# One step of a hybrid recurrence/attention block: where the chunk sums of the modulation, the second set of keys and the weight parts stand in the order of work

## Chip, cores and metric

The kernel runs on one core of one Trainium2 chip, as one launch. The metric is the device time of that launch in microseconds (us). Three runs of the kernel before gave 2032.13, 2034.22 and 2036.62 us; the median, 2034.22 us, is the time to compare with.

The core's engines work side by side, each through its own queue in order: TensorE (PE in the profile, with its weight loads as PEld), VectorE (DVE), ScalarE (ACT), GpSimd (POOL), and SyncE (SP), whose queue issues most of the DMAs. Matrix products go to PSUM, of which this kernel has eight banks in use under three tags: three "g", three "s" and two "t".

## What is computed

One trunk layer for 256 context tokens and 1024 latent tokens, width 1024, all in float32. Cut to what matters here:

```python
m = silu(cond) @ w_ada + b_ada            # 6 x 1024 modulation values, for two conditions
h = rms_norm(x) * (1 + sc1) + sh1
z = h @ w_in                              # 1024 x 5376: recurrence, attention, gates
q, k = rms_norm per head (+ rotary)
o_a = softmax(q k^T / 8) v                # 8 heads, 2 key heads, latents see 512 cached keys too
s   = dec * s + k_end^T v                 # gated recurrence, 4 heads, two directions, by chunks
o_h = intra + inter, rms_norm, silu gate
x   = x + g1 * ((gate0 * o_h @ w_ho + gate1 * o_a @ w_ao) @ w_out)
x   = x + g2 * (relu(norm2(x) @ w_ff1) ** 2 @ w_ff2)
```

The vector `m` has 48 columns of 128 values for each condition. Sixteen of them (`sh1`, `sc1`) are needed at the start; the other thirty-two are made beside the attention and the recurrence.

## The kernel before

Each float32 product is made of three passes in a rounded format (high by high, high by low, low by high), so every operand is first split into a high and a low part: one ACT copy and one DVE subtraction (`split`, L318 and L319). In the part of the kernel that the change touches, PE is given its order by hand: what the program issues first, PE does first. DVE, ACT, POOL and SP are ordered by a planner that follows the program's order, raised or lowered by `tc.high_priority(offset=...)` and held back by `tc.issue_after(x)`, which keeps an instruction's place behind x.

**Filler.** The projection `z = h @ w_in` for eighteen column groups of 256 is a generator, `with_ada`, that issues three matmuls (a "triple", L351 to L353 or L368 to L370) at each step. `attention` and `hgrn` draw on it between their own steps, by shares of the total and not by time. Groups 3, 4, 8 and 9 have 80 triples each (token-major), the others two halves of 24.

**Attention.** Thirty-two latent units of six steps, then eight context units of one step, 200 steps in all. `events` gives each action of a unit a place on one axis: scores (L856), exponentials (L868), at each step `trans` (four transposes L888 of the probabilities into a bank "t", split by ACT and DVE at L891), and later `value` (L902, L903). All events are sorted by place and carried out with filler between them. The keys of the second group of heads are loaded (`load_k`) 8.95, 8.85 and 7.9 steps ahead of step 96.

**Chunk sums.** Twelve chunks of two columns of `m` are made beside the filler's groups 1 to 9. `begin` loads a chunk of `w_ada` (a tile of ring "wraw", two places, shared with the groups' weights) and lets POOL multiply and add it up into `ACC`, one pair of buffers for all chunks (`ada_sum`, L197 to L204). `end` puts eight small matmuls with ones (L209) on PE, into a bank "t", and an ACT copy (L211); a third action puts one transpose (L215) into another bank "t" and a DVE addition (L217). All three stand at shares of a group: in a token-major group `begin` at 0.02, `end` at 0.45 and the last at 0.49, then again 0.5, 0.93 and 0.97; in the others 0.25, 0.93 and 0.97. The group after the current one is loaded at 0.05 of a token-major group.

**Recurrence.** Twenty-four units (4 heads, two directions, three token tiles). Each has a long preparation on DVE, POOL and ACT, scores (L1133), `states_` with the products L1145 into a bank "s" and a chain of two or four updates on DVE (L1154), `out`, `keys_t` and, for every second direction, `gate`. Filler runs between them.

**Weight parts.** `Group.part` splits a half of a group's weights with its place held behind `behind`, a pair that `trans` sets to the last ACT and DVE splits of the probabilities. Nothing sets `behind` in the recurrence. The split weights lie in ring "wsp" with six places, three halves.

## Time and profile before

| | |
|---|---|
| median of three runs | 2034.22 us |
| the profiled execution's own time | 2033.12 us |
| its span in the profile | 2031.1 us |
| PE busy | 1999.8 us, 98% of the span |
| DVE busy | 1346.1 us, 66% |
| ACT busy | 941.9 us, 46% |
| POOL busy | 584.7 us, 29% |
| granted TensorE clock, mean | 0.998 |

The span is counted from the first to the last instruction of the program; 2.0 us of the execution lie around it. Attention runs from about 160 to 700 us, the recurrence from about 700 to 980 us. A busy share is counted from starts and modelled ends of matmuls, which overlap by up to 0.2 us, so a pause of PE shorter than that doesn't show as idle.

### The profile page before, as it was taken

The page shows a single profiled execution, that of the slowest core. Times are in us where ns is not written, and L with a number is a line of the kernel's source. Part 1 is how long each engine was busy: PE and PEld are TensorE (multiplying, and loading weights), DVE is VectorE, ACT ScalarE, POOL GpSimd, SP SyncE. Part 2 cuts the span into 40 slices and gives each one's busy share as a digit, 9 for nine tenths or more (in the row PEclk, how much of TensorE's full clock was granted, in tenths as well). Part 3 has the DMA queues.
Part 4 walks back from the last instruction along what each step waited for, and adds up shares of the span by engine and source line. Part 5 has one row for each costly group of instructions (what it writes and reads, how often), then busy time and mean ns, then how long its engine had stood idle before and what let it go on. Part 6 is the DMA issues. An engine that isn't in the chain of part 4 may idle for free.

```text
span 2031.1 us, 32983 instructions
## 1 busy us (share of the span) xinstructions
PE 1999.8 (98%) x12183; PEld 1729.0 (85%) x12183; DVE 1346.1 (66%) x2469; ACT 941.9 (46%) x1974; POOL 584.7 (29%) x651
## 2 busy tenths in 40 slices
PE   7999999999999999999999999999999999999998
PEld 5898899988889988888888889988888888888886
DVE  5955656555665789887445535876666666577786
ACT  4735565555565423333412236754554544333443
POOL 1571337523325555554022101222212200000120
PEclk9999999999999999999999999999999999999999
DMA  9472221322122355553844435854444489455764
GB/s 319 136 226 76 79 81 63 110 91 77 55 73 92 123 180 157 187 160 125 261 135 148 148 110 160 258 173 147 157 153 148 154 313 351 126 173 174 233 237 134
DMA packets 222562, 320.00 MB, mean 158 GB/s; under 512 B 19097, under 2 KB 140737, under 8 KB 222401
## 3 DMA queue, kind: packets, MB, share of 16 engines
q1 hardware_dynamic: 209920, 277.99, 42.9%
q0 software_dynamic: 12480, 39.91, 5.3%
q8 instruction: 96, 1.57, 0.3%
q14 instruction: 66, 0.53, 0.1%
HBM read 232.05 MB, written 85.78 MB: 156 GB/s over the span
## 4 chain that ended last, share of the span: by engine, by line
PE 92%; DVE 3%; DMA 2%; ACT 1%; issue 1%; SPq 0%; POOL 0%; POOLq 0%; DVEq 0%; ACTq 0%
PE ps_g L351 8%; PE ps_g L353 8%; PE ps_g L352 8%; PE ps_s L856 4%; PE ps_t L888 4%; PE ps_g L903 2%; PE ps_g L368 2%; PE ps_g L902 2%; PE ps_g L369 2%; PE ps_g L370 2%; PE ps_g L1844 2%; PE ps_g L1845 2%; PE ps_g L1843 2%; PE ps_s L1683 2%; PE ps_s L1684 2%; PE ps_s L1682 2%
## 5 line engine op out<-in xcount | busy, mean ns | idle before, releaser
L351 PE MATMUL ps_g<-hs,wsp 128*128 128x512 f32 (+1 forms) x896 | 322.2, 360 | 0.0
L353 PE MATMUL ps_g<-hs,wsp 128*128 128x512 f32 (+1 forms) x896 | 309.2, 345 | 0.0
L352 PE MATMUL ps_g<-hs,wsp 128*128 128x512 f32 (+1 forms) x896 | 309.0, 345 | 0.0
L318 ACT ACTIVATE wsp<-wraw 128x512 fp32r<-128x512 f32 (+1 forms) x186 | 116.7, 667 | 227.3 <-PE ps_g L352 95.9
L319 DVE TENSOR_TENSOR wsp<-wraw,wsp 128x512 fp32r<-128x512 f32 (+1 forms) x186 | 149.0, 822 | 89.6 <-ACT wsp L318 89.3
L857 DVE TENSOR_REDUCE mx<-ps_s 128x1 f32<-128x512 f32 (+1 forms) x208 | 137.6, 667 | 105.1 <-PE ps_s L856 103.6
L891 DVE TENSOR_TENSOR pTl<-ps_t,pTh 128x512 fp32r<-128x512 f32 x200 | 136.4, 684 | 88.8 <-ACT pTh L891 88.5
L353 PEld LDWEIGHTS ps_g<-hs,wsp 128*128 128x128 f32 x896 | 169.3, 189 | 21.6
L351 PEld LDWEIGHTS ps_g<-hs,wsp 128*128 128x128 f32 x896 | 169.6, 189 | 19.7 <-issue 4.8
L352 PEld LDWEIGHTS ps_g<-hs,wsp 128*128 128x128 f32 x896 | 169.9, 190 | 14.4
L891 ACT ACTIVATE pTh<-ps_t 128x512 fp32r<-128x512 f32 x200 | 118.8, 603 | 125.1 <-PE ps_t L888 124.7
L318 ACT ACTIVATE ah<-ar 128x640 fp32r<-128x640 f32 (+1 forms) x112 | 80.9, 723 | 187.5 <-PE ps_g L1844 102.3
L868 ACT ACTIVATE pexp<-ps_s,ngm 128x512 f32<-128x512 f32 (+1 forms) x208 | 137.6, 671 | 46.3 <-DVE ngm L861 46.0
L319 DVE TENSOR_TENSOR ah<-ar,ah 128x640 fp32r<-128x640 f32 (+1 forms) x112 | 92.0, 822 | 76.6 <-ACT ah L318 76.3
L856 PE MATMUL ps_s<-Kl,Ql 128*128 128x512 f32 (+1 forms) x416 | 130.2, 411 | 1.1 <-DMA Kl<-KS 1.0
L888 PE MATMUL ps_t<-ident,pexp 128*128 128x128 f32 x800 | 120.3, 273 | 1.9 <-ACT ev L211 1.3
L368 PE MATMUL ps_g<-wsp,hs 128*128 128x256 f32 x400 | 116.3, 291 | 0.0
L370 PE MATMUL ps_g<-wsp,hs 128*128 128x256 f32 x400 | 112.8, 282 | 0.0
L369 PE MATMUL ps_g<-wsp,hs 128*128 128x256 f32 x400 | 112.7, 282 | 0.0
L888 PEld LDWEIGHTS ps_t<-ident,pexp 128*128 128x128 f32 x800 | 94.1, 140 | 12.5 <-ACT ev L211 2.1
L903 PE MATMUL ps_g<-pTl,Vl 128*128 128x256 f32 x400 | 104.0, 282 | 0.2
L902 PE MATMUL ps_g<-pTh,Vl 128*128 128x256 f32 x400 | 104.1, 282 | 0.0
(448 smaller groups left out, 5411.9 us busy)
## 6 DMA issues: line engine op xcount, KB each, us to landing
ar<-AF SPq DMA_DIRECT2D x112, 320.0 KB, 3.4
wraw<-in_w_ff SPq DMA_DIRECT2D x32, 1024.0 KB, 6.4
wr<-in_w_ff SPq DMA_DIRECT2D x128, 256.0 KB, 4.6
wraw<-in_w_in SPq DMA_DIRECT2D x18, 1024.0 KB, 5.6
wraw<-in_w_ada SPq DMA_DIRECT2D x16, 1024.0 KB, 5.3
AF<-a POOLq DMA_DIRECT2D x48, 256.0 KB, 2.7
AF<-t POOLq DMA_DIRECT2D x48, 256.0 KB, 2.4
wa<-in_w_ada SPq DMA_DIRECT2D x32, 256.0 KB, 5.9
```

What stands on the lines that cost most here:

```text
L318: s_.activation(hi, raw, AF.Copy)
L319: return v.tensor_tensor(lo, raw, f32(hi), op=ALU.subtract)
L351: pe.matmul(out, hi[:, k, :], mh, start=(first and k == 0), stop=False)
L352: pe.matmul(out, hi[:, k, :], ml, start=False, stop=False)
L353: pe.matmul(out, lo[:, k, :], mh, start=False, stop=(last and k == kcs - 1))
L368: pe.matmul(po[:, bb, :], mh[:, off:off + P], wh[:, k % 4, :], start=(k == 0), stop=False)
L369: pe.matmul(po[:, bb, :], mh[:, off:off + P], wl[:, k % 4, :], start=False, stop=False)
L370: pe.matmul(po[:, bb, :], ml[:, off:off + P], wh[:, k % 4, :], start=False, stop=(k == KC - 1))
L856: pe.matmul(pq[:, 0:n], self.qh[:, q0:q0 + P], K[self.g][var][self.kts[i]], start=(var == 0), stop=(var == 1))
L888: pe.transpose(pt[:, a, j * P:(j + 1) * P], self.Ps[j][i][:, b * P:(b + 1) * P], ident)
L891: behind[:] = s_.activation(hi, pt, AF.Copy), v.tensor_tensor(lo, pt, f32(hi), op=ALU.subtract)
L902: pe.matmul(pv[:, 0:256], V[self.g][kg][:, b, :], hi[:, a, :], start=(k == 0), stop=False)
```

## The change

Three edits.

1. `end` no longer puts its matmuls on PE: it leaves them in `waiting`. A new event, `beat`, stands 0.01 ahead of `trans` at steps 0 and 3 of each latent unit and at the step of each context unit. A beat carries out one thing: the transpose that is left from the beat before, or else the eight matmuls of the oldest chunk waiting. If a `begin` came while a chunk was waiting, it is put off (`starts`) and carried out in the same beat, behind the matmuls. After the attention all that is left is carried out.
2. The second set of keys is loaded 9.95, 9.85 and 8.95 steps ahead of step 96; the first set as before.
3. `behind` is also set by each update of a state (L1154) and by the addition that ends `out` in the second direction (L1177), together with `copied[0]`, the last copy of transposed keys on ACT. So in the recurrence the splits of weights stand behind these.

```diff
@@ Unit.events
             for p2 in range(self.nstep):
+                if p2 % 3 == 0:
+                    out.append((p2 - 0.01, beat, ()))
                 out.append((p2, self.trans, (p2,)))
@@ attention
-                    events += [(s0 - a, load_k, (u.g, kg)) for kg, a in enumerate((8.95, 8.85, 7.9))]
+                    events += [(s0 - a, load_k, (u.g, kg)) for kg, a in enumerate((9.95, 9.85, 8.95) if s0 else (8.95, 8.85, 7.9))]
@@ HUnit.states_
-                    v.scalar_tensor_tensor(dst, st, self.dec[:, b:b + 1], kv[:, b, :], op0=ALU.mult, op1=ALU.add)
+                    behind[:] = copied[0], v.scalar_tensor_tensor(dst, st, self.dec[:, b:b + 1], kv[:, b, :], op0=ALU.mult, op1=ALU.add)
@@ HUnit.out
-                v.tensor_tensor(o[:, 0:nb], po[:, 0:nb], fwd.o[:, 0:nb], op=ALU.add)
+                behind[:] = copied[0], v.tensor_tensor(o[:, 0:nb], po[:, 0:nb], fwd.o[:, 0:nb], op=ALU.add)
@@ build
+    waiting, starts, lasts = [], [], []
+
+    def beat():
+
+        if lasts:
+            lasts.pop()()
+        elif waiting:
+            lasts.append(waiting.pop()())
+            if starts:
+                starts.pop()()
+
@@ with_ada
                 def begin():
-                    late.append(ada_sum(ahead.pop(0), ACC))
+                    if waiting:
+                        starts.append(begin)
+                    else:
+                        late.append(ada_sum(ahead.pop(0), ACC))
 
                 def end():
-                    late.append(late.pop()())
-                acts = [(0.02, begin), (0.45, end), (0.49, lambda: late.pop()())] if grp.tok else []
+                    waiting.append(late.pop())
+                acts = [(0.02, begin), (0.45, end)] if grp.tok else []
                 if nxt and nxt in groups[:10]:
-                    acts += [(0.5 if grp.tok else 0.25, begin), (0.93, end), (0.97, lambda: late.pop()())]
+                    acts += [(0.5 if grp.tok else 0.25, begin), (0.93, end)]
@@ build
     attention(fz)
+    while waiting or lasts:
+        beat()
```

## The prediction, made before the changed kernel was run

> **What bounds the kernel now.** I read the page's busy shares first, then the chain that ended last, then the stretches of attention and recurrence, then what PE waited for.

> ```profile
> PE 1999.8 (98%) x12183; PEld 1729.0 (85%) x12183; DVE 1346.1 (66%) x2469; ACT 941.9 (46%) x1974; POOL 584.7 (29%) x651
> ...
> PE 92%; DVE 3%; DMA 2%; ACT 1%; issue 1%; SPq 0%; POOL 0%; POOLq 0%; DVEq 0%; ACTq 0%
> ```
> ```profile
> 160.00:700.00 540.00, 535.19 (x3779) 487.27 (x3778) 325.50 (x622) 313.86 (x753) 216.08 (x221) 1.00 0.26 83
> 700.00:980.00 280.00, 278.03 (x2264) 236.68 (x2263) 228.89 (x535) 88.03 (x226) 144.00 (x155) 1.00 0.51 162
> ```
> ```profile
> PE ps_s L1145 <- issue: 2.0, 2, 1.2
> ...
> PE ps_t L209 <- DVE pTl L891: 1.3, 1, 1.3
> ...
> PE ps_t L888 <- ACT ev L211: 1.3, 3, 0.4
> PE ps_s L856 <- DMA Kl<-KS: 1.0, 2, 0.9
> ...
> PE ps_t L888 <- DVE modc L217: 0.5, 2, 0.3
> ...
> PE ps_t L215 <- ACT ev L211: 0.2, 1, 0.2
> ```

> PE is the bound. In the stretch of attention (160 to 700 us) it idles 4.8 us, in the recurrence 2.0 us; the change takes no work off PE, so what it can win lies in these two stretches. The waits name nearly all of it: 3.3 us at seven places around the chunk sums (1.3 + 1.3 + 0.5 + 0.2), 1.0 us for keys, 2.0 us ahead of L1145. The true loss is a little more, because the modelled end of a matmul overlaps the next one:

> ```profile
> 528.79 0.27 PE L352 MATMUL ps_g<-hs,wsp 128*128 128x256 f32 x1
> 528.91 0.28 PE L353 MATMUL ps_g<-hs,wsp 128*128 128x256 f32 x1
> 530.52 0.30 PE L209 MATMUL ps_t<-sums,ones 128*32 128x128 f32 x2 [1.33 <-DVE pTl L891]
> ```

> From start to start this is 1.61 us where the neighbour of that shape started 0.12 before, so 1.49 is lost and 1.33 shown: 0.16 more at each place. That makes about 4.4 us for the sums (3.3 + 7 x 0.16), 1.3 for the keys, 2.3 before L1145. **8.0 us, 0.4%, is the most that can be won.**

> **Part 1a, the sums' old waits: 4.4 us go, about 2.4 come back.** A beat puts the sum's bank "t" between two `trans`, and there are two such banks. Whether `trans` then waits depends on how long before it the previous `trans` was split off. One unit's step 3 and the next unit's step 0, with the DVE split of the step before each:

> ```profile
> 282.84 0.60 PE L888 MATMUL ps_t<-ident,pexp 128*128 128x128 f32 x4
> 282.96 0.68 DVE L891 TENSOR_TENSOR pTl<-ps_t,pTh 128x512 fp32r<-128x512 f32 x1
> ...
> 289.45 0.68 DVE L891 TENSOR_TENSOR pTl<-ps_t,pTh 128x512 fp32r<-128x512 f32 x1
> 290.98 0.60 PE L888 MATMUL ps_t<-ident,pexp 128*128 128x128 f32 x4
> ```

> At step 0 the previous split ended at 290.13, 0.85 us before: both banks are free and a beat costs nothing. At step 3 it ends at 283.64, 0.8 us after `trans` began; with a beat ahead, `trans` waits for that or for the beat's own bank, whichever is first. What the latter costs, the trace shows:

> ```profile
> 272.67 0.66 PE L888 MATMUL ps_t<-ident,pexp 128*128 128x128 f32 x4 [0.26 <-DVE modc L217]
> ```

> 0.26 and the hidden 0.16 are 0.4 us lost; behind the ACT copy (1.3 us at three places) it is 0.6. I take 0.5. Setting the old places of the twelve sums against the beats, I find about ten of the 24 beats at a step 3. Half of these waiting 0.5 gives 2.4 us; the ends are 0 and 5. Net gain 2.0.

> **Part 1b, the last sum: a new wait of about 7.6 us.** The beat makes a sum late, and a sum that is late holds up the next chunk on POOL, since `ACC` is one buffer.

> ```profile
> 657.51 0.62 POOL L197 TENSOR_TENSOR sums<-wraw,ada_l 128x256 f32<-128x256 f32 x1 [9.18 <-PE ps_t L209]
> ...
> 677.88 0.74 POOL L204 TENSOR_TENSOR pvt<-wraw 128x256 f32<-128x256 f32 x1
> ```

> A chunk takes POOL 21.1 us (657.51 to 678.62), and starts 0.5 us after the sum before it. For the others, whose places lie farther apart, there is room. For the last there isn't:

> ```profile
> 652.94 0.60 PE L888 MATMUL ps_t<-ident,pexp 128*128 128x128 f32 x4
> ...
> 657.01 0.30 PE L209 MATMUL ps_t<-sums,ones 128*32 128x128 f32 x2
> ...
> 664.51 0.60 PE L888 MATMUL ps_t<-ident,pexp 128*128 128x128 f32 x4
> ...
> 681.78 0.30 PE L209 MATMUL ps_t<-sums,ones 128*32 128x128 f32 x2
> ...
> 682.95 0.60 PE L888 MATMUL ps_t<-ident,pexp 128*128 128x128 f32 x4
> ```

> The eleventh sum's `end` is at 657.01, behind the beat at the step 3 of 652.94. The next beat is that of the first context unit, at 664.51, 7.5 us later. The last sum's `end` is at 681.78; its beat follows at 682.95. So POOL would have 683.0 - 665.0 = 18.0 us for 21.1 us of work: at least 3.1 us late.

> The ring of raw weights makes it worse. In that stretch the filler does so many triples:

> ```profile
> 657.20:661.20 4.00, 1.89 (x7) 1.32 (x7) 1.00 0.33 93
> 661.20:663.00 1.80, 0.86 (x4) 0.57 (x3) 1.00 0.43 155
> ```

> The `end` at 0.93 of group 8 stands at triple 75 of 80, so the last `begin` (0.02 of group 9) comes at the 7th triple behind it, before 661.2, and group 10's load (0.05) at the 10th, before 663.0 (one of the four is counted twice). The sum before still waits, so this `begin` is put off to 664.51, past the load. The two now take their ring places in the other order. Which places these are:

> ```profile
> 648.36 0.39 SPq L101 DMA_DIRECT2D wraw<-in_w_ada  x1
> ...
> 664.14 0.49 SPq L101 DMA_DIRECT2D wraw<-in_w_in  x1
> ```
> ```profile
> 662.06 2.05 DVE L319 TENSOR_TENSOR wsp<-wraw,wsp 128x512 fp32r<-128x512 f32 x2
> ```
> ```profile
> wraw<-in_w_ada SPq DMA_DIRECT2D x16, 1024.0 KB, 5.3
> ```

> Today the chunk is loaded at 648.36 and group 10's weights at 664.14, as soon as DVE has split group 9's last weights (662.06 + 2.05). Swapped, the chunk's load goes at 664.14, lands 5.3 later at 669.4, and POOL ends at 690.5. PE stands at L209 from 683.0 to 690.6: 7.6 us (3.1 if the places don't swap). Behind it in PE's queue stand the next transposes, the last values and all filler; ACT and DVE wait for those. SP's queue only exchanges two loads.

> **The clock.** A pause of that length costs more than itself:

> ```profile
> 16.60:20.00 3.40, 1.70 (x23) 1.08 (x22) 0.94 (x3) 1.89 (x4) 0.00 (x0) 1.00 1.09 349
> 20.00:23.40 3.40, 3.40 (x9) 2.64 (x9) 2.68 (x4) 1.54 (x3) 0.00 (x0) 0.50 1.09 360
> ...
> 2027.00:2031.00 4.00, 0.00 (x0) 0.00 (x0) 0.00 (x0) 0.00 (x0) 0.00 (x0) 0.51 0.36 133
> ```

> After 3.4 us in which PE was half idle the granted clock was 0.50 for the next 3.4 us, with PE fully busy; and at the end of the kernel it is 0.51 from 2027 on. 3.4 us at half speed lose 1.7 us. I add 1.7; the ends are 0 and 3.4. [...]

> **Part 2, the keys: 1.3 us go.**

> ```profile
> 395.38 2.49 SPq L101 DMA_DIRECT2D Kl<-KS  x4
> ```
> ```profile
> 401.83 0.47 PE L856 MATMUL ps_s<-Kl,Ql 128*128 128x512 f32 x1 [0.86 <-DMA Kl<-KS]
> ```

> The last four loads are issued from 395.38 to 397.87 and PE waits for them at 401.83. One step is about 2.7 us (540 us, 200 steps), more than the 1.3 lost. The cover is a free place in ring "X", where two exponentials now come behind the keys; if SP finds none earlier, nothing is won. Bounds 0 and 1.3; I take 1.3.

> **Part 3, weight parts behind updates: 2.3 us go, about 1.5 come.**

> ```profile
> 788.76 2.12 DVE L319 TENSOR_TENSOR wsp<-wraw,wsp 128x512 fp32r<-128x512 f32 x2
> 790.80 0.34 DVE L1154 SCALAR_TENSOR_TENSOR ust<-ust,udec,ps_s 128x128 f32<-128x128 f32 x1
> ```
> ```profile
> 777.64 1.06 PE L1145 MATMUL ps_s<-uv,ukt 128*128 128x128 f32 x8
> ```
> ```profile
> L319 DVE TENSOR_TENSOR wsp<-wraw,wsp x30: 626/681/1541, 704.0 to 969.9; 128x512 fp32r<-128x512 f32 x30
> ```

> Two splits of a later half's weights stand ahead of the last update of a chain, and PE's next L1145 waits for the bank. Held back, they leave the chain. But then a half's splits come only when the filler asks for them, half a half ahead of use, behind the updates of that moment. Thirty splits, two to a half, are 15 halves in 280 us, so that lead is some 9 us. And DVE runs late: this chain's products were done by 778.7 and its last update at 791.1. DVE is busy 228.89 of 280 us here. A few waits of PE for weights, 0.5 us each, are likely: 1.5 in all; ends 0 and 7. Net gain 0.8.

> **Sum.** Against the profiled execution's 2033.12 us (span 2031.1 and 2.0 around it): -2.0 - 1.3 - 0.8 + 7.6 + 1.7 = +5.2, so 2038.3. The median of the runs, 2034.22, is 1.1 above that execution: **2039.4 us**. A measurement of this kernel can tell 0.2% (4.1 us) from no change, so this is just beyond it.

> **Rivals.**
> *The ring doesn't swap.* [...] For it: the swap hangs on the 1.5 us between 663.0 and the beat. Chance 0.13.
> *No new wait, faster.* If PE takes the eleventh sum before about 661.5 and its load is not put off, POOL is done by 683 and only the gains stay: 2034.2 - 4.1 = 2030.1, a little less where step 3 costs less. It decides at the beat of 664.51: 3 us earlier and nothing waits. Against it: places are shares of the filler, and don't drift. Chance 0.20.
> *The weights become the wait.* Three or four halves of the recurrence each 2 us late: 5.5 more, 2045. For it: DVE's lag of 12 us against a lead of 9. Chance 0.12.
> *The clock stays whole*: 2037.7. Chance 0.09.
> *The forecast*: 0.46, from 2036 to 2043.

> **Chances.** Slower by over 0.2% (above 2038.3): three quarters of the forecast and the weights, 0.46. Within: the rest of the forecast 0.12, no swap 0.13, whole clock 0.09, the dearer end of no wait 0.03, 0.37. Faster: 0.17. The range takes in the end of no wait and most of the late weights: 2029 to 2044.

> **What would show it.** One L209 near 683 with a wait for POOL of 7 to 8 us, the last load of a chunk behind a load of group 10, and a stretch of granted clock below 1 behind it; L888 waits gone at step 0 and some 0.4 at step 3; no wait at L856 near 400; no split between updates of one chain, and perhaps L351 waiting for DVE. If L209 waits nowhere, the count of triples or of POOL's time is wrong.

## The result, and the profile after

The changed kernel takes 2049.67 us (median of six runs, 2046.01 to 2051.3) against 2033.49 us of the kernel before, measured beside it (six runs, 2032.13 to 2036.62). The ratio is 1.0076, with a 95% interval of 1.0066 to 1.0087: 16 us slower. The direction was forecast; the time lies 5.7 us above the top of the range. The profiled execution took 2051.27 us, its span is 2049.4 us (2031.1 before).

The busy shares and the chain that ended last, from the page of the changed kernel:

```profile
PE 2004.6 (98%) x12183; PEld 1732.5 (85%) x12183; DVE 1344.3 (66%) x2469; ACT 941.5 (46%) x1974; POOL 582.7 (28%) x651
...
PE 90%; DVE 5%; DMA 2%; POOL 1%; issue 1%; ACT 1%; SPq 0%; POOLq 0%; DVEq 0%; ACTq 0%
```

PE does the same 12183 matmuls, but its busy time grew by 4.8 us although no matmul was added: some of them ran slower (L353 on 128x512 took 0.39 us at 869.30, with the clock at 1.00, and 0.63 at 876.85, with the clock at 0.50). POOL is now in the chain. The same stretches as before (window, its length, then busy time of PE, PEld, DVE, ACT and POOL, granted clock, DMA share, GB/s):

```profile
160.00:700.00 540.00, 524.02 (x3666) 475.48 (x3665) 317.10 (x602) 308.74 (x744) 210.11 (x218) 0.99 0.25 81
700.00:980.00 280.00, 276.09 (x2252) 235.69 (x2251) 227.47 (x534) 85.13 (x211) 144.35 (x153) 0.99 0.47 149
```

PE idles 16.0 us in the stretch of attention (4.8 before) and 3.9 us in the recurrence (2.0 before), and the clock is 0.99 in both, where it was 1.00 before. What PE waited for (total, times, longest; the added lines of the diff move L888 to L890, L891 to L893, L1145 to L1147 and L1154 to L1156):

```profile
PE ps_t L209 <- POOL pvt L204: 9.3, 1, 9.3
...
PE ps_s L1147 <- issue: 3.5, 2, 3.1
PE ps_t L890 <- DVE modc L217: 3.1, 4, 1.5
...
PE ps_t L209 <- POOL sums L200: 2.0, 1, 2.0
...
PE ps_t L890 <- ACT ev L211: 0.8, 2, 0.4
```

The wait for keys is gone. Of the sums' old waits one stands where it stood (0.4, near 207 us); the others are gone, and there are new ones: behind POOL (L209) and at step 3 (L890). The waits at the state's products (L1147) are longer than before. Each has its own history.

**The last sum.** SP's loads of raw weights around it, from the timeline of SP:

```profile
652.52 0.39 SPq L101 DMA_DIRECT2D wraw<-in_w_in  x1
...
664.26 0.53 SPq L101 DMA_DIRECT2D wraw<-in_w_ada  x1
```

Before, the chunk's load stood first (648.36) and the group's weights second (664.14). They have swapped, and the second place of the ring comes free at the same time as before. POOL, which cannot begin without the chunk (the figure in brackets is idle time ahead of the instruction, with what ended it):

```profile
672.27 0.61 POOL L197 TENSOR_TENSOR sums<-wraw,ada_l 128x256 f32<-128x256 f32 x1 [19.79 <-DMA wraw<-in_w_ada]
...
693.40 0.72 POOL L204 TENSOR_TENSOR pvt<-wraw 128x256 f32<-128x256 f32 x1
```

And PE, behind which everything queues:

```profile
682.18 0.28 PE L370 MATMUL ps_g<-wsp,hs 128*128 128x256 f32 x1
684.48 0.41 PE L209 MATMUL ps_t<-sums,ones 128*32 128x128 f32 x4 [2.03 <-POOL sums L200]
694.18 0.64 PE L209 MATMUL ps_t<-pvt,ones 128*32 128x128 f32 x4 [9.28 <-POOL pvt L204]
```

11.3 us are shown; with the hidden 0.16 at each of the two waits, PE lost 11.6. Why the load took 8.0 us to be usable stays open. In the trace's DMA view the traffic falls from 295 GB/s (669.0 to 669.5) to 24 and 26 (670 to 671 and 671 to 672), which suggests that it is the end of the load that drags.

**The clock.** The half clock lasts 13.65 and 6.82 us in this trace, four and two times 3.41. Windows of 3.41 us, laid so that their edges meet those of the half clock (the third figure from the right is the clock):

```profile
681.99:685.40 3.41, 0.88 (x8) 0.40 (x7) 0.33 (x1) 0.00 (x0) 3.17 (x5) 1.00 0.11 38
685.40:688.81 3.41, 0.00 (x0) 0.00 (x0) 0.00 (x0) 0.00 (x0) 3.41 (x2) 0.50 0.00 0
...
692.23:695.64 3.41, 1.46 (x9) 1.09 (x9) 0.00 (x0) 0.28 (x1) 1.81 (x2) 0.50 0.10 14
695.64:699.05 3.41, 3.41 (x18) 3.41 (x17) 1.89 (x3) 2.01 (x4) 0.00 (x0) 0.50 0.89 293
...
869.72:873.13 3.41, 1.34 (x6) 0.75 (x5) 3.41 (x8) 0.94 (x2) 3.17 (x3) 1.00 0.37 140
873.13:876.54 3.41, 2.39 (x10) 2.32 (x11) 3.41 (x6) 1.18 (x5) 1.59 (x2) 0.50 0.08 32
876.54:879.95 3.41, 3.41 (x10) 2.64 (x9) 3.41 (x12) 0.00 (x0) 2.21 (x4) 0.50 0.44 127
```

Each stretch ends with its last line here. At half the clock a product of 128x512 starts 0.43 us after its neighbour (876.85 to 877.28), at the whole clock 0.23 (869.30 to 869.53). From these two I estimate that half the clock costs half of the time that PE is busy in it: (1.46 + 3.41) / 2 = 2.4 us behind the last sum, and (2.39 + 3.41) / 2 = 2.9 us in the recurrence, where no drop was foreseen.

**The sums at step 3.** Beats at step 0 of a latent unit wait nowhere. At step 3 four transposes of sums cost 3.1 us, two sums' matmuls 0.8. The dearest of the four, on PE and then on DVE:

```profile
407.88 0.30 PE L215 MATMUL ps_t<-ident,ev 128*128 128x128 f32 x1
409.67 0.63 PE L890 MATMUL ps_t<-ident,pexp 128*128 128x128 f32 x4 [1.49 <-DVE modc L217]
```
```profile
408.25 0.68 DVE L1032 SCALAR_TENSOR_TENSOR ze<-ze,ps_g 128x512 f32<-128x512 f32 x1
408.84 0.68 DVE L893 TENSOR_TENSOR pTl<-ps_t,pTh 128x512 fp32r<-128x512 f32 x1
409.44 0.15 DVE L217 TENSOR_TENSOR modc<-ps_t,cols 128x4 f32<-128x4 f32 x1
```

The view names the addition of four columns (L217), which frees the beat's own bank, because it is the last to end before `trans`. The cheapest of the four shows that `trans` didn't wait for it; DVE, then PE's loads of weights:

```profile
639.38 0.68 DVE L893 TENSOR_TENSOR pTl<-ps_t,pTh 128x512 fp32r<-128x512 f32 x1
640.03 0.16 DVE L217 TENSOR_TENSOR modc<-ps_t,cols 128x4 f32<-128x4 f32 x1
640.18 0.31 PEld L890 LDWEIGHTS ps_t<-ident,pexp 128*128 128x128 f32 x3 [0.42 <-PE ps_t L215]
```

`trans` begins to load at 640.18, before the addition ends at 640.19. What has ended is the split of the step before (L893), at 640.06, 0.12 us earlier; at the other three places this distance is 0.12 us as well. There are two banks "t". With a transpose in between, `trans` takes the bank of the `trans` before it and waits for that one's split. At 283.67 and 608.82 this split stands on DVE behind one operation of 0.68 us (L857), at 409.67 behind two (L857 and L1032).

**The recurrence.** The last update of a chain (L1156) ends late because the preparation behind which it stands on DVE started late. From the timelines of DVE, SP and PE, and the waits of SP between 838 and 872:

```profile
859.06 0.68 DVE L319 TENSOR_TENSOR wsp<-wraw,wsp 128x512 fp32r<-128x512 f32 x1
...
866.52 1.23 DVE L1064 TENSOR_TENSOR_SCAN ucp<-R,uf 128x512 f32<-128x512 f32 x1 [2.35 <-DMA uf<-FD]
...
873.72 0.33 DVE L1156 SCALAR_TENSOR_TENSOR ust<-ust,udec,ps_s 128x128 f32<-128x128 f32 x1
```
```profile
859.76 0.38 SPq L101 DMA_DIRECT2D wraw<-in_w_ada  x1
860.20 0.63 SPq L101 DMA_DIRECT2D uf<-FD  x1
```
```profile
SPq L101 <- DVE wsp L319: 7.9, 1, 7.9
```
```profile
874.15 2.05 PE L1147 MATMUL ps_s<-uv,ukt 128*128 128x128 f32 x8 [3.09 <-issue]
```

Read from the top: the split of weights, now held behind a chain of updates, frees its place of raw weights at 859.74. SP stands at the load that takes this place, and has waited 7.9 us for it. The recurrence's own load `uf` stands behind on the same queue; DVE idles 2.35 us for it; the whole preparation and the updates behind it move; PE waits 3.09 us at the products, and the clock halves.

Set against the prediction's terms, on the two profiled spans: keys -1.3; sums' old waits -4.4 and new ones +4.9 (3.1 + 0.8 and 6 x 0.16); last sum +11.6; clock +2.4 and +2.9; waits at the state's products +1.5 (3.5 + 2 x 0.16, against 2.3). That makes 17.6 of the 18.3 us between the spans. The other 0.7 isn't traced to the change: a wait at L621, near the start of the kernel, of 1.4 before and 2.1 after, is of that size.

### The profile page after: what moved, and what is told of

The parts are those of the page before. It is cut to its first block, busy times and chain, and to the rows that moved or that the text cites. A ratio compares the mean times of both kernels' runs of the same rounds, so it can differ in the third digit from the quotient of the medians.

```text
span 2049.4 us, 32995 instructions
## 1 busy us (share of the span) xinstructions
PE 2004.6 (98%) x12183; PEld 1732.5 (85%) x12183; DVE 1344.3 (66%) x2469; ACT 941.5 (46%) x1974; POOL 582.7 (28%) x651
## 4 chain that ended last, share of the span: by engine, by line
PE 90%; DVE 5%; DMA 2%; POOL 1%; issue 1%; ACT 1%; SPq 0%; POOLq 0%; DVEq 0%; ACTq 0%
PE ps_g L351 8%; PE ps_g L353 7%; PE ps_g L352 7%; PE ps_t L890 4%; PE ps_s L856 4%; PE ps_g L1862 2%; PE ps_g L1863 2%; PE ps_g L1861 2%; PE ps_g L905 2%; PE ps_g L904 2%; PE ps_s L1702 2%; PE ps_s L1700 2%; PE ps_s L1701 2%; PE ps_g L368 2%; PE ps_g L370 2%; PE ps_g L369 2%
## 5 line engine op out<-in xcount | busy, mean ns | idle before, releaser
L351 PE MATMUL ps_g<-hs,wsp 128*128 128x512 f32 (+1 forms) x896 | 322.9, 360 | 0.0
L353 PE MATMUL ps_g<-hs,wsp 128*128 128x512 f32 (+1 forms) x896 | 310.1, 346 | 0.2 <-DVE wsp L319 0.2
L352 PE MATMUL ps_g<-hs,wsp 128*128 128x512 f32 (+1 forms) x896 | 309.8, 346 | 0.0
L857 DVE TENSOR_REDUCE mx<-ps_s 128x1 f32<-128x512 f32 (+1 forms) x208 | 137.4, 667 | 118.6 <-PE ps_s L856 117.4
L319 DVE TENSOR_TENSOR wsp<-wraw,wsp 128x512 fp32r<-128x512 f32 (+1 forms) x186 | 148.7, 822 | 83.7 <-ACT wsp L318 83.4
L893 DVE TENSOR_TENSOR pTl<-ps_t,pTh 128x512 fp32r<-128x512 f32 x200 | 136.4, 684 | 95.6 <-ACT pTh L893 95.2
L353 PEld LDWEIGHTS ps_g<-hs,wsp 128*128 128x128 f32 x896 | 169.7, 189 | 22.3 <-DVE wsp L319 0.6
L351 PEld LDWEIGHTS ps_g<-hs,wsp 128*128 128x128 f32 x896 | 170.0, 190 | 19.7 <-issue 4.8
L352 PEld LDWEIGHTS ps_g<-hs,wsp 128*128 128x128 f32 x896 | 170.3, 190 | 14.6
L893 ACT ACTIVATE pTh<-ps_t 128x512 fp32r<-128x512 f32 x200 | 118.4, 602 | 116.5 <-PE ps_t L890 115.5
L319 DVE TENSOR_TENSOR ah<-ar,ah 128x640 fp32r<-128x640 f32 (+1 forms) x112 | 92.0, 822 | 74.4 <-ACT ah L318 74.0
L856 PE MATMUL ps_s<-Kl,Ql 128*128 128x512 f32 (+1 forms) x416 | 129.9, 411 | 0.0
L890 PE MATMUL ps_t<-ident,pexp 128*128 128x128 f32 x800 | 121.2, 274 | 4.3 <-DVE modc L217 3.1
L890 PEld LDWEIGHTS ps_t<-ident,pexp 128*128 128x128 f32 x800 | 93.8, 140 | 16.9 <-issue 3.9
## 6 DMA issues: line engine op xcount, KB each, us to landing
wraw<-in_w_ff SPq DMA_DIRECT2D x32, 1024.0 KB, 6.4
wraw<-in_w_in SPq DMA_DIRECT2D x18, 1024.0 KB, 5.4
wraw<-in_w_ada SPq DMA_DIRECT2D x16, 1024.0 KB, 5.6
```

What stands on the lines that cost most here:

```text
L319: return v.tensor_tensor(lo, raw, f32(hi), op=ALU.subtract)
L351: pe.matmul(out, hi[:, k, :], mh, start=(first and k == 0), stop=False)
L352: pe.matmul(out, hi[:, k, :], ml, start=False, stop=False)
L353: pe.matmul(out, lo[:, k, :], mh, start=False, stop=(last and k == kcs - 1))
L856: pe.matmul(pq[:, 0:n], self.qh[:, q0:q0 + P], K[self.g][var][self.kts[i]], start=(var == 0), stop=(var == 1))
L890: pe.transpose(pt[:, a, j * P:(j + 1) * P], self.Ps[j][i][:, b * P:(b + 1) * P], ident)
```

## The experiments

The theory (A): each of the three places named above is a cost of its own, by its own mechanism, and the second edit does what it says. The rivals were that the sums cost by their beats and not by the last chunk's load; that the order of the ring doesn't matter; and that the third edit costs by its splits (on DVE, or as waits of PE for weights) and not by SP's queue. All diffs are against the kernel before or after, as named.

**The parts alone.** First, only the sums (the kernel after, without the keys' edit and without `behind`):

```diff
-                    behind[:] = copied[0], v.scalar_tensor_tensor(dst, st,
+                    v.scalar_tensor_tensor(dst, st,
...
-                behind[:] = copied[0], v.tensor_tensor(o[:, 0:nb], po
+                v.tensor_tensor(o[:, 0:nb], po
...
-enumerate((9.95, 9.85, 8.95) if s0 else (8.95, 8.85, 7.9))
+enumerate((8.95, 8.85, 7.9))
```

> Only the beats for the chunk sums; keys and weight parts as before. Theory A (the late last sum makes the loss): one L209 near 682 waits 10 to 12 us for POOL, the granted clock is at half for a stretch behind it, some L890 wait at step 3 for 4 to 5 us in all; 2033.5 plus 11 to 14, so 2045 to 2048. Theory B (the loss comes from the weight parts in the recurrence): 2032 to 2035.

Measured: 2044.77 us (2043.17 to 2044.96) against 2033.43, ratio 1.0053 (1.0041 to 1.0066). Its waits of PE:

```profile
PE ps_t L209 <- POOL pvt L204: 9.3, 1, 9.3
PE ps_t L890 <- DVE modc L217: 3.1, 4, 1.5
...
PE ps_t L209 <- POOL sums L200: 1.2, 1, 1.2
```

The first edit carries the two waits at L209 and those at step 3 by itself.

The keys alone (second edit in the kernel before):

> Only the second keys one step earlier. Theory A: the wait at L856 near 401 is gone and nothing takes its place, 1.3 us less, 2032.2. Theory B (the place in ring X is only taken from an exponential): no change, 2033.5.

Measured: 2031.38 us (2030.38 to 2033.06), ratio 0.999 (0.9981 to 0.9999). No wait for `Kl` is left in its trace. 2.0 us by the medians, where the trace's wait was worth 1.3.

The weight parts alone (third edit in the kernel before):

> Only the weight parts behind the state updates. Theory A (SP stands at a load of raw weights, the recurrence's loads queue behind it, and a pause of over 3 us lowers the clock): a wait at L1147's place of about 3 us and a half clock of 3.4 to 6.8 us, 3 to 6 us more, 2036.5 to 2039.5; the old waits of 1.2 and 0.7 us gone or moved. Theory B (that wait only came of the other timing behind the late sum): 2 us less, 2031.5.

Measured: 2035.61 us (2034.28 to 2037.52), ratio 1.0011 (1.0002 to 1.002): 2.2 us slower, 0.9 below the range that the theory gave. From its timelines of SP, DVE and PE:

```profile
845.49 0.38 SPq L101 DMA_DIRECT2D wraw<-in_w_ada  x1
845.92 0.62 SPq L101 DMA_DIRECT2D uf<-FD  x1
```
```profile
852.14 1.23 DVE L1062 TENSOR_TENSOR_SCAN ucp<-R,uf 128x512 f32<-128x512 f32 x1 [2.25 <-DMA uf<-FD]
```
```profile
859.77 1.13 PE L1145 MATMUL ps_s<-uv,ukt 128*128 128x128 f32 x8 [1.94 <-issue]
```

The same chain as in the changed kernel, some 14 us earlier because the stall at 682 is missing. In the kernel before the same two loads went at 824.13 and 838.25, and the scan had no wait. The pause is 1.9 us where about 3 was expected (3.09 in the changed kernel, with the clock at 0.50 behind it), and the clock stays whole (1.00 from 840 to 880): that is what the miss consists of. The parts alone make 11.3 - 2.0 + 2.2 = 11.5 us; together they make 16.2. The rest is the second half clock (2.9, which neither part has alone), a longer first one (2.4 against 1.5: there PE is busy only 2.91 us of it) and a longer stand at L209 (11.3 against 10.4): 4.7.

**Who takes the ring's place.** The kernel after, in which a `begin` that is put off still takes its place and its load at once; only POOL's work waits for the beat:

```diff
-                        starts.append(begin)
+                        ci = ahead.pop(0)
+                        raw = wraw(I["w_ada"], KC, ci * P)
+                        starts.append(lambda: late.append(ada_sum(ci, ACC, raw)))
```

> All of the change, but a begin that is put off still takes its place in the ring of raw weights at once; only POOL's sums are put off. Theory A (two of the three causes of the late sum are the swapped places and the slow load): the last L209 waits 3 to 4 us instead of 11.5, too short or just long enough for one window at half clock; 8 to 11 us less than the changed kernel, 2039 to 2042. Theory B (POOL itself is late, the order of the loads doesn't matter): as the changed kernel, 2049.7.

Measured: 2039.94 us (2038.84 to 2041.16), ratio 1.0031 (1.002 to 1.0043).

```profile
686.01 0.64 PE L209 MATMUL ps_t<-pvt,ones 128*32 128x128 f32 x4 [3.59 <-POOL pvt L204]
```

With its places unswapped the last sum waits 3.6 us; the prediction gave 3.1 for this case. The medians of the two kernels differ by 9.7 us, their spans by 10.9 (2049.4 and 2038.5). Of the latter 7.9 is at L209 (11.3 against 3.6 as shown, and 0.16 hidden at one place more) and 2.9 is the second half clock, which this trace doesn't have although L1147 waits 2.84 us in it (1.00 from 860.10 to 866.92). Behind L209 both have a half clock, at 2.4 us and, here, at 1.7 (0.50 from 686.02 to 689.43, PE busy throughout); waits of PE for weights at L353 give 0.7 back (0.9 here, 0.2 there).

**When the eleventh sum is taken.** The kernel after with one beat more, ahead of the last step of the last latent unit, so that the eleventh sum is taken earlier and the last load isn't put off:

```diff
-                if p2 % 3 == 0:
+                if p2 % 3 == 0 or (s0, p2) == (186, 5):
```

> All of the change and one more beat, ahead of step 5 of the last latent unit, so that the eleventh sum goes near 660 and the last begin is not put off. Theory A (the last sum waits because the one before it went at 664): no L209 waits for POOL over 0.5 us and the granted clock stays whole near 690; 12 to 15 us less than the changed kernel, 2035 to 2037.5. Theory B (POOL's chunk is too long for the place in any case): a wait of 3 us or more stays, 2040.

Measured: 2035.51 us (2033.78 to 2036.59), ratio 1.0009 (1.0 to 1.0018). No L209 waits for POOL any more. One beat that takes the eleventh sum at 661.23 and not at 663.87 takes 14 us away, as the rival "no new wait" had said of this point. What stays is the waits at step 3 and the recurrence (2.8 at L1147, and a half clock of one window, 0.50 from 859.30 to 862.71).

**The sums mended.** Matmuls of a sum only at steps 0 and 3, its transpose only at steps 0 and 4, and the added beat of the run before; keys as in the change, weight parts as before:

```diff
-                if p2 % 3 == 0:
-                    out.append((p2 - 0.01, beat, ()))
+                if p2 in (0, 3, 4) or (s0, p2) == (186, 5):
+                    out.append((p2 - 0.01, beat, (p2 != 3, p2 != 4)))
...
-    def beat():
+    def beat(last=True, first=True):
         if lasts:
-            lasts.pop()()
-        elif waiting:
+            if last:
+                lasts.pop()()
+        elif waiting and first:
```

> Keys as changed, weight parts as before, the extra beat of the last unit, and at step 3 a beat that only does the eight matmuls, with the transposes moved to a new beat at step 4. Theory A (3.3 of the 4.7 us lost at step 3 come of transposes whose bank waits for DVE's addition): L890 waits of 1.5 us or less in all, keys' wait gone, no wait for POOL; 2028.5 to 2030.5, 3 to 5 us less than before. Theory B (any beat between two transposes costs about 0.4 us): 2031.5 to 2033.

Measured: 2027.95 us (2026.5 to 2030.13), ratio 0.9975 (0.9964 to 0.9986): 5 us faster than before. Its waits of PE between 160 and 980 us are these and no others:

```profile
PE ps_s L1147 <- issue: 1.7, 2, 1.0
PE ps_t L890 <- ACT ev L211: 0.8, 2, 0.4
PE ps_t L890 <- PE ps_t L209: 0.2, 1, 0.2
```

The transposes at step 4 wait nowhere. The split of the step before is done there: at the first of them that used to wait it ends at 284.72, and the transpose starts at 284.77. The theory had put the old wait down to the addition and not to the split; the result is the same for both. The keys are 1.3 to 2.0 of the 5 us. So chunk sums at set places do win most of what the old waits cost; the change's choice of places, and its last chunk, gave it back.

**Which halves of the weight parts.** The third edit alone, but held behind updates only for a group's first half, and then only for its second:

```diff
-                    if x is not None:
+                    if x is not None and (self.c0 < GL or i == 0):
```

> Kernel before, with only the first half of a gate group's weights held behind the state updates; the second half, whose split frees the place in the ring of raw weights, is free. Theory A (the loss comes of SP standing at the raw load behind the second half's split): SP's wait for these splits falls to 3 us or less near 830 to 860, the scan of the next unit waits for no load, L1145's wait of 1.9 is gone or under 0.8; 2031.5 to 2033.5. Theory B (the splits' own time on DVE, moved into the busy stretch, makes the chain late): a wait of 1.5 us or more stays, 2035.

> Kernel before, with only the second half of a gate group's weights held behind the state updates. Theory A (SP stands at the raw load): SP's long wait for the split and the scan's wait for its load stay, L1145 waits 1.5 us or more once; 2034.5 to 2036.5. Theory B (the splits' own time on DVE): half as many moved, 2034.

Measured: first halves 2030.48 us (2028.9 to 2035.74), ratio 0.9991 (0.9982 to 0.9999), with no wait at L1145 at all; second halves 2036.13 us (2034.4 to 2038.71), ratio 1.0014 (1.0005 to 1.0023), with a wait of 1.5 at L1145 and a new one of 1.8 at L902, behind which the clock halves for one window (0.50 from 678.40 to 681.81). Here a gate group's other half is held behind nothing, not even behind `trans` at the end of the attention, where the new wait stands (676.96); so the second of these runs changes more than the halves of the recurrence. A half's raw weights are given back when the *second* half is split, so this is what the theory says; but it doesn't yet tell SP's queue from the splits.

**SP's queue, a test that missed.** The third edit alone with `uf` and `uq` loaded from POOL's queue, and beside it the kernel before with that alone:

```diff
-            dma(f[:, 0:n], FD[d][h][t])
-            dma(q[:, 0:n], QD[h][t])
+            store(f[:, 0:n], FD[d][h][t])
+            store(q[:, 0:n], QD[h][t])
```

> The third edit alone, with the recurrence's loads uf and uq issued from POOL's queue, so that they no longer stand behind SP's wait for a place for raw weights. Theory A (the third edit loses only through uf and uq late behind SP's load of raw weights): the scan L1064 near 850 waits for no DMA, the wait of L1145 near 860 falls from 1.94 to 1.2 or less, and against the control e11 this kernel is level or faster by up to 3 us (ratio of the two 0.9985 to 1.0005). Rival (the late splits cost by themselves, on DVE or in PE's waits for weights): the wait of L1145 stays 1.5 to 2, and the kernel is 2 to 3 us slower than e11. What POOL's queue costs shows in e11 against before; estimate 0 to 4 us slower, since POOL is busy 144 of the 280 us there.

> The control of e10: the kernel before with uf and uq loaded from POOL's queue and no other edit. Both theories: 2033 to 2038, by how long POOL's own work keeps the loads back.

Measured: 2048.29 us (2044.43 to 2049.62) with the third edit, 2035.42 us (2034.02 to 2037.09) without. 12.9 us apart: neither level, as the theory said, nor 2 to 3 us, as the rival did. The wait of L1145 is gone, but PE waits elsewhere: in the recurrence it idles 9.4 us, 8.2 more than in the control. The granted clock is 0.96 from 780 to 860 and 0.97 from 860 to 920. That is about two windows of half clock, to some 813.3 (0.50 from 808.00 to 812.60, 0.89 from there to 816.00), and about one from some 878.2. PE is busy some 8.2 us in them, which is 4.1 us lost by the estimate above. The two make 12.3 of the 12.9. From the waits of PE between 700 and 985, then the timelines of DVE and PE:

```profile
PE ps_g L353 <- DVE wsp L319: 6.8, 2, 4.4
```
```profile
807.12 0.34 DVE L1154 SCALAR_TENSOR_TENSOR ust<-ust,udec,ps_s 128x128 f32<-128x128 f32 x1
807.38 1.28 DVE L319 TENSOR_TENSOR wsp<-wraw,wsp 128x512 fp32r<-128x512 f32 x2
```
```profile
808.11 0.79 PE L353 MATMUL ps_g<-hs,wsp 128*128 128x512 f32 x1 [4.40 <-DVE wsp L319]
```

On POOL's queue `uf` starts behind POOL's own work (at 804.74, behind two L1084 that began at 802.73), which the control has too. The split, tied by the third edit to the last update (807.12), starts only at 807.38, and PE stands for it 4.4 us. So the test didn't single out SP's queue; it showed a second danger of the edit, the rival "the weights become the wait", which comes true when the updates are late by another cause.

**SP's queue, alone.** The third edit alone; the four loads of a chunk of `w_ada` in the recurrence have their place behind the latest `uq`, and nothing else is touched:

```diff
-            dma(q[:, 0:n], QD[h][t])
+            lastq[0] = dma(q[:, 0:n], QD[h][t])
...
-                todo.append(ada_cols(PS("g"), wraw(I["w_ada"], KC, ci * P), ci))
+                with tc.issue_after(lastq[0].ins):
+                    raw = wraw(I["w_ada"], KC, ci * P)
+                todo.append(ada_cols(PS("g"), raw, ci))
```

> The third edit alone, and one thing changed on SP's queue: the loads of the recurrence's four chunks of w_ada (one of which stood at 845.49 in the trace of the third edit alone, with uf behind it) have their place behind the latest loads uf and uq. Nothing else moves on PE or DVE. Theory A (the third edit's loss comes through uf and uq that stand behind SP's wait for a place for raw weights): uf is issued near 838, the scan L1064 near 852 waits for no DMA, the wait of L1145 near 861 falls from 1.94 to 1.2 or less, and the time is 2031 to 2034 (the third edit alone: 2035.61, its control 2033.4). Rival (the late splits cost by themselves): the wait of L1145 stays at 1.5 to 2 and the time at 2035 to 2037. Rival B (the chunk's load is now late): PE waits for DMA at L178, 1 us or more, and the time is 2035 or more.

Measured: 2032.0 us (2029.85 to 2032.59) against 2033.82, ratio 0.9989 (0.998 to 0.9998). From the timeline of SP, and the stretch of the recurrence:

```profile
839.35 0.32 SPq L101 DMA_DIRECT2D uf<-FD  x1
...
848.25 0.42 SPq L101 DMA_DIRECT2D wraw<-in_w_ada  x1
```
```profile
700.00:980.00 280.00, 279.38 (x2272) 238.12 (x2271) 227.14 (x536) 87.83 (x227) 146.41 (x155) 1.00 0.52 163
```

`uf` goes 6.6 us earlier, the scan near 850 doesn't wait for it, no wait at L1145 is left, and PE idles 0.6 us in the recurrence (3.7 with the third edit alone, 2.0 before). The other place of these loads on SP's queue turns 2.2 us of loss into 1.8 of gain. Each of the two ratios lies only just clear of 1; it is the trace, in which the waits are gone, that carries the argument. Of the late splits by themselves 0.6 is left, one wait for weights; PE waits for no late chunk.

**Both mended parts together.** The mended sums, the keys, and the third edit for first halves:

> The mended kernel of e6 (keys loaded ahead, sums' matmuls at beats 0 and 3, their transposes at beat 4, one more beat ahead of step 5 of the last latent unit) with the third edit added for the first half of each gate group alone. Theory A (what the third edit loses is lost at SP's load of raw weights, which only the second halves' late splits hold up): no wait at the state's store of 1.5 us or more, no half clock in the recurrence, and the gain of e7 adds to e6: 2027.95 - 2.3 to - 3, so 2024.5 to 2026.5. Rival (the two gains are one and the same pause, which e6 has already lost): 2027.5 to 2029. Rival B (the late splits of the first halves trip the clock in the new phase of the windows): 2030 or more, with half clock between 600 and 900.

Measured: 2026.84 us (2026.62 to 2027.73) against 2034.72, ratio 0.9961 (0.9947 to 0.9974). The median is 0.3 us above the range that the theory gave, and 0.7 below the rival's. The trace has no wait of L1147 and no half clock in the recurrence (1.00 from 700 to 980), so the two gains are different pauses; but the interval overlaps with that of the mended sums alone, so how much the second adds isn't settled. It is the fastest kernel here: 7.9 us faster than the kernel before by the medians of its round, in which the kernel before stood at 2034.72 (2033.2 to 2033.8 in the other rounds), and 6.0 by the profiled spans (2025.1 and 2031.1). The mended sums with the hold of the last experiment were not tried.

## Why the prediction was right in its direction and wrong in its size

The forecast for the span was +5.2 us, and 17.6 are accounted for. The terms below make up the difference: 2.5 at the sums' waits, 4.0 at the last sum, 3.6 in the clock and 2.3 in the weight parts.

- **The bound: right.** What could be won was put at 8.0 us; the best kernel here won 7.9 by the medians, 6.0 by the spans.
- **Part 1a (sums' old waits): place right, size wrong.** Beats at step 0 cost nothing and those at step 3 cost something, as forecast, and ten of them stood at step 3. But six waited for 4.9 us, not five for 2.4, and nothing was won. The step that failed is the price, "0.5". Of the two banks that `trans` could wait for it priced the beat's own, from places where the addition of the columns was next on DVE or the ACT copy came first. For the two sums' matmuls that held (0.6 each). Behind the four transposes `trans` waited for the other bank, the split of the step before. The prediction had that price in hand: it read a split that ends 0.8 us after `trans` began (283.64), and the beat at this very step lost 0.84 (0.68 shown, 0.16 hidden). Where one operation more stood ahead of the split, 1.65 were lost. The far end of this term, 5, is nearly what was measured.
- **Part 1b (last sum): mechanism right in every link, size 7.6 where it was 11.6.** The swap of the two loads, the time of the last load (664.14 forecast, 664.26 measured) and the stand of PE at L209 all came. Two terms were too small. The load was taken at its median, 5.3 us, and POOL started 8.0 us behind it; the chain on POOL was taken as 21.1 and took 21.9 (672.27 to 694.12), with two memsets of `R` (0.6 us) now in it. Together 3.5; PE also came to L209 some 0.7 earlier than forecast. The bound of this term was never drawn: 7.6 stood with a lower end and no upper one.
- **Clock: 1.7 forecast, 2.4 + 2.9 by the estimate above.** The first drop came and lasted four windows, of which PE worked in two. The second, in the recurrence, wasn't foreseen: waits there were priced at 0.5 us each, and one of 3.09 came.
- **Part 2 (keys): right.** 1.3 forecast, the wait gone, 2.0 by the runs.
- **Part 3 (weight parts): wrong in sign.** A net gain of 0.8 was forecast; the part alone loses 2.2 us, and in the whole change 4.4 (1.5 of waits and 2.9 of clock). The step that failed is the sentence "SP's queue only exchanges two loads", which was written for the first edit and never asked of the third. Holding a split back holds back the place it frees, the load that waits for this place, and the loads behind that on SP (7.9 us in the changed kernel, with `uf` behind). The expected removal of 2.3 is real: with SP's queue put right, all of that wait is gone. The return was looked for in waits of PE for weights, and of those there is 0.2 in the changed kernel; they are the dearer rival only where updates are late (6.8 with `uf` on POOL's queue).
- **Rivals.** "No new wait" named the point of decision, 3 us at the beat of 664.51; 2.6 were enough in the run with one more beat. "The ring doesn't swap" stood on the wait of 3.1 in Part 1b; it then measured 3.6, and the clock halved behind it (0.50 from 686.02 to 689.43).

All four misses have the same sign. In the largest of them a load slower than its median and a longer chain on POOL stand one behind the other, so they add and don't average out.

## What to carry to other kernels

When an instruction is held back, follow the buffer that it frees: who loads into that place, on which queue, and what stands behind that load. On SP's queue the 7.9 us that one load waited in the changed kernel were paid by the load behind it as well (`uf`, issued at 860.20, right behind the one at 859.76); the place of four loads was the whole difference between two kernels, one of which lost 2.2 us and the other won 1.8. And give work with a fixed place its slack from the other side: ask when the next piece needs it, at the last place in the row and not at a typical one.

## What the runs showed of the hardware

```profile
674.99:678.40 3.41, 1.66 (x14) 1.45 (x14) 3.41 (x10) 2.01 (x7) 1.42 (x2) 1.00 0.00 0
678.40:681.81 3.41, 3.41 (x19) 3.41 (x18) 1.85 (x6) 2.02 (x6) 3.33 (x2) 0.50 0.37 128
859.30:862.71 3.41, 1.91 (x13) 1.48 (x12) 2.52 (x5) 0.74 (x5) 1.39 (x2) 1.00 0.00 0
862.71:866.12 3.41, 3.41 (x21) 2.95 (x20) 3.31 (x5) 0.96 (x3) 2.72 (x3) 1.00 0.47 146
```

The lower pair is the other side: 1.91 us busy, and the clock stays at 1.00. The kernel before had 1.70 of 3.40 busy ahead of its only drop in the midst of work. So windows with 0.01 to 1.70 us of work were followed by half the clock, in all of these cases but one (the first 16 us stand apart: there the view gives 1.00 also behind idle windows, as in the changed kernel behind 2.73 to 6.15 with 0.00 us of work), whether the idle time is one pause or two (2.03 and 0.50 us ahead of 685.40). The one case that stands against a sharp line: with the load kept PE was busy 1.62 us from 860.10 to 863.51, the edges carried over 51 windows from the drop at 686.02, and the clock stayed at 1.00 to 866.92. What tells this window from that with 1.66 isn't known. In the traces of the changed kernel, the sums alone, the load kept, the added beat and the second halves, no drop between 160 and 990 us followed a window with 1.8 us of work or more. On the way back, a window with 2.39 us of work at half clock (changed kernel, from 873.13) was followed by another at 0.50, while one with 2.91 (sums alone, from 692.93) was followed by 0.99.
